# Gated delta rule: block inverses, key products and root chains in PSUM, banks regrouped, gated output in one product

## The chip, the cores and the metric

The kernel runs on one core of a Trainium2 chip. The metric is the device time of one execution in microseconds. A core has these engines: PE (matrix products, with a weight load, PEld, ahead of each), DVE (elementwise and reductions), ACT (activation functions and copies), POOL (elementwise) and SP (here only a queue that issues transfers). Each takes its instructions in the order in which the build wrote them down. Two memories are on the core: SBUF, and PSUM with eight banks of 512 fp32 values per partition. PE writes its results to PSUM; DVE and ACT read and write both memories, POOL and the transfers only SBUF.

## The reference

Four layers on 256 tokens of width 1024 in fp32. The change lies in the first layer's mixer, a gated delta rule with 8 key heads and 16 value heads of 128, in chunks of 64 tokens:

```
q = silu(conv(h @ w_q)); k = ...; v = ...      # q, k: 8 heads, each used by 2 value heads
q, k = l2_norm(q), l2_norm(k)                  # x * rsqrt(sum(x*x) + 1e-6)
a = where(strict, (k*beta) @ k.T * decay, 0)
t_inv = triangular_solve(eye + a, eye)         # lower triangular, unit diagonal
u, w = t_inv @ (v*beta), t_inv @ (k*beta*exp(g))
qk = q @ k.T * decay
for each chunk:                                # scan over the chunks
    v_new = u_c - w_c @ state
    out = qd_c @ state + qk_c @ v_new
    state = state * exp(gl_c) + kd_c.T @ v_new
o = out * rsqrt(mean(out*out) + 1e-6) * out_gain * silu(z)
x = x + o @ w_out
```

## The kernel before

All weights are fp32 and stream in chunks of 128 x 1024. ACT rounds a chunk to its high part (wh, L465), then DVE (L470) or POOL (L468), as a fixed pattern in the stage's plan says, subtracts that from the raw chunk to get the low part (wl). Three products of high and low parts make one fp32 product on PE (L481 and L484, or L493 to L495).

A planner orders the instructions of each engine at build time, from the order of the program, priorities, its own estimates of durations, and the memory slots that are free. At run time the order is fixed. A tile pool is a set of slots; a tile that finds none free waits until the slot's last user is done.

The stage of the gated delta rule runs from the start to about 350 us. In program order: the z gates for the first group of four value heads; the small projections for beta and decay; `project` for k, then for q (four steps each: PE projects into the pool `acc`, four banks of PSUM, DVE convolves in three steps at L726, ACT applies silu, squares go to PE again, which sums them per head into the tile pss); `rsqrt` of the sums of k, 32 values per partition; `rb` = rk * beta, which PE transposes (ps_rk, L884) and which goes through DRAM to be a row on all partitions.

Key products: for two token halves n and two head groups b PE multiplies k by itself (ps_kk, L902), ACT scales each head into an SBUF tile kkn (L905), DVE multiplies it by the decay row into UU (L909). The diagonal blocks of 32 x 32 go through DRAM into a tile A that has one block per partition. `tri_inverse` inverts all 128 blocks at once on DVE, 31 rounds of two instructions, a product into stmp (L1826) and a subtraction from T (L1827):

```
for i in range(31):
    r, m = 31 - i, i // parts + 1
    tv = tmp[:, : r * m].rearrange("p (c j) -> p c j", c=r)
    V.tensor_tensor(tv, A[:, i, i + 1 :]..., T[:, i, :m]..., op=ALU.mult)
    V.tensor_tensor(T[:, i + 1 :, :m], T[:, i + 1 :, :m], tv, op=ALU.subtract)
```

T and its transpose return through DRAM (dTR). While DVE works on this, PE goes on with q, the key-query products (ps_kq, L961, scaled by ACT into kkn at L964, multiplied on DVE at L967), the v projections (`values`, with PE transposes ps_v at L943), and the z gates. A string in the plan gives the order of what follows, `+` for parts that alternate:

```
order='v0 z1 v1 z2 l0 v2 l1+s0 v3 l2+s1 z3 l3+s2 s3'
```

v are the values, z the gates, l the levels, which join the 32 x 32 inverses to blocks of 128 (`join_blocks`), s the scans with `out_norm` at their end. All of the tiles pss, ps_rk, ps_kk, ps_kq, ps_v and those of levels and scan share one PSUM pool with the tag `mm` and four banks. In `out_norm` POOL multiplies the gate zs by the scan's output (L1048) while DVE works out the rsqrt, and DVE scales each head (L1050). `_gdn_out` transposes that (ps_ot, L1073) and multiplies by w_out.

Of the kernel before, what the change touches and what calls it, by code (L numbers as in the profile page):

```python
# [41 lines left out]
        gk=4,  # L42
        tag='mm',
        order='v0 z1 v1 z2 l0 v2 l1+s0 v3 l2+s1 z3 l3+s2 s3',
# [331 lines left out]
def run(g):  # L376
    for _ in g:
        pass
# [3 lines left out]
class Prog:  # L382
# [114 lines left out]
    def rsqrt(self, out, src, shape, scale, eps, pool=None, tag=None, bufs=1, key=""):  # L497
# [18 lines left out]
        for i in range(3):  # L516
# [5 lines left out]
            nc.vector.scalar_tensor_tensor(out if i == 2 else y, t, 1.5, y, op0=ALU.add, op1=ALU.mult)  # L522

    def load_row(self, src, shift=None, queue=None):

        self.row = self.xp.tile([128, D + 128], F32, name="row", tag="row")
        queue = queue or self.nc.sync
        queue.dma_start(self.row[:, :D], src.partition_broadcast(128))
        if shift is not None:
            self.nc.gpsimd.memset(self.row[:, D:], 0.0)  # L530
            queue.dma_start(self.row[0:8, D:], shift)
# [197 lines left out]
    def gdn(self, x):  # L729
        nc, tc, ap = self.nc, self.tc, self.ap  # L730
        with ExitStack() as outer:
            self.psum(outer)
            for t in range(2):
                self.stats(x, t, [self.pa.tile([128, 512], F32, name="junk", tag="acc") for _ in range(2)])
            self.prefetch(*((self.ap["g_z"][c], CW) for c in range(self.plan["pre"])))
            self.load_first(outer, "fi0")
            dr = outer.enter_context(tc.tile_pool(name="g_dram", bufs=1, space=DRAM))
            go = outer.enter_context(tc.tile_pool(name="g_o", bufs=1, reuse_waits="tile"))
            vb = [[go.tile([128, 4, 128], F32, name=f"vb{n}{g}") for g in range(4)] for n in range(2)]
            zs = [[go.tile([128, 4, 128], F32, name=f"zs{n}{g}") for g in range(4)] for n in range(2)]  # L740
            rq = go.tile([128, 2, 16], F32, name="rq")
            inner = ExitStack()
            gi = inner.enter_context(tc.tile_pool(name="g_i", bufs=1, reuse_waits="tile"))
            scan_last = self._gdn_core(x, dr, gi, vb, rq, zs, inner)
            self._gdn_out(x, zs, scan_last, inner)

    def _gdn_core(self, x, dr, gi, vb, rq, zs, inner):
# [42 lines left out]

        run(gates(0))
        phase_a = ExitStack()
        pA = phase_a.enter_context(tc.tile_pool(name="g_a", bufs=1, reuse_waits="tile"))
# [34 lines left out]

        def project(dst, c0, mt0):

            pss = self.pm.tile([128, 2, 16], F32, name="pss", tag="mm")
            sqs = []
# [20 lines left out]
            sums()  # L853
            yield pss

        with tc.tile_pool(name="g_rk", bufs=1, reuse_waits="tile") as pr:
            rrow = pr.tile([16, S], F32, name="rrow")
            kp, qp = project(kc, 0, 8), project(qc, 4, 0)
            for _ in range(self.plan["gk"]):
# [18 lines left out]
            fl = lambda a: a.rearrange("p n h -> p (n h)")  # L878
            self.rsqrt(fl(rk), fl(next(kp)), (128, 32), 1.0, 1e-6, pool=pr)
            rb = pr.tile([128, 2, 16], F32, name="rb")  # L880
# [13 lines left out]
        for n in range(2):  # L894
# [3 lines left out]
            for b in range(2):  # L898
                ps = self.pm.tile([128, 4, 128], F32, name="ps_kk", tag="mm")
                for k in range(4):  # L900
                    a = kc[:, b * 4 + k, n * 128 : n * 128 + 128]
                    nc.tensor.matmul(ps[:, k, :], a, a, start=True, stop=True)  # L902
                kk = gi.tile([128, 4, 128], F32, name="kkn", tag="kkn", bufs=2)
                for k in range(4):
# [9 lines left out]
        for g in range(4):  # L914
            u = UU[:, 8 * g : 8 * g + 8]
            nc.gpsimd.affine_select(u, u, [[0, 8], [1, 128]], ALU.not_equal, 1.0, base=0, channel_multiplier=-1)

        A = pA.tile([128, 32, 32], F32, name="sA")
        T = pA.tile([128, 32, 32], F32, name="sT")
        tmp = pA.tile([128, 256], F32, name="stmp")  # L920
        nc.sync.dma_start(A.rearrange("p j c -> p (j c)"), dA)
        self.tri_inverse(128, A, T, tmp)
        nc.sync.dma_start(dTR[0], T.rearrange("p c j -> p (c j)"))
        nc.vector.tensor_copy(A, T.rearrange("p c j -> p j c"))
        nc.sync.dma_start(dTR[1], A.rearrange("p c j -> p (c j)"))

# [22 lines left out]
        with tc.tile_pool(name="g_rq", bufs=1, reuse_waits="tile") as pr:  # L949
            for _ in range(3):  # L950
                next(qp)
            next(v0)
            self.rsqrt(fl(rq), fl(next(qp)), (128, 32), 1.0, 1e-6, pool=pr)
            nc.vector.tensor_scalar(rq, rq, 128.0 ** -0.5, None, op0=ALU.mult)
            nc.vector.tensor_tensor(rq2, rq, rq, op=ALU.mult)
        for n in range(2):
            for b in range(2):
                ps = self.pm.tile([128, 4, 128], F32, name="ps_kq", tag="mm")
                for k in range(4):
                    sl = (slice(None), b * 4 + k, slice(n * 128, n * 128 + 128))  # L960
                    nc.tensor.matmul(ps[:, k, :], kc[sl], qc[sl], start=True, stop=True)  # L961
                kq = gi.tile([128, 4, 128], F32, name="kkn", tag="kkn", bufs=2)
                for k in range(4):
# [5 lines left out]

        pB = inner.enter_context(tc.tile_pool(name="g_b", bufs=1, reuse_waits="tile"))  # L970
        TR = [pB.tile([128, 2, 8, 128], F32, name=f"TR{i}") for i in range(2)]
        E = pB.tile([128, 8, 64], F32, name="lev_e")
        for t in (*TR, E):
            nc.gpsimd.memset(t, 0.0)
        t2k = lambda nm: pB.tile([128, 4, 128], F32, name=nm, tag="b2k", bufs=5)
        TG = self.plan["tag"]
        bank = lambda nm, tag="mm": self.pm.tile([128, 4, 128], F32, name=nm, tag=tag)
        def mm4(lhs, rhs, nm, tag="mm"):
            ps = bank(nm, tag)
            for u in range(4):  # L980
# [16 lines left out]
        def scan(g):  # L997
            hs = slice(4 * g, 4 * g + 4)
            bc = lambda c: c.unsqueeze(2).to_broadcast([128, 4, 128])

            vn = t2k("vn")
            nc.scalar.copy(vn, mm4(TR[g % 2][:, 1, 0:4], vb[0][g], "ps_vn", TG))
            kd = t2k("kd")
            ps = bank("ps_kd", TG)
            for i in range(2):
# [4 lines left out]
            st = t2k("st")  # L1010
            nc.scalar.copy(st, mm4(kd, vn, "ps_s", TG))
            nc.scalar.copy(vb[0][g], mm4(GT[0][:, hs], vn, "ps_o", TG))
            yield

            ps = bank("ps_ks", TG)
            for i in range(2):
# [3 lines left out]
            nc.gpsimd.tensor_tensor(vb[1][g], vb[1][g], ks, op=ALU.subtract)  # L1020
            ps = bank("ps_qs", TG)
            for i in range(2):
# [4 lines left out]
            vn1 = t2k("vn")  # L1027
            nc.scalar.copy(vn1, mm4(TR[g % 2][:, 1, 4:8], vb[1][g], "ps_vn", TG))
            yield
            nc.vector.tensor_tensor(vb[1][g], mm4(GT[1][:, hs], vn1, "ps_o", TG), qs, op=ALU.add)  # L1030
            yield
# [3 lines left out]
        def out_norm(g):  # L1035

            hs = slice(4 * g, 4 * g + 4)
            for n in range(2):
# [8 lines left out]
                nc.vector.tensor_tensor(rs, rs, rq[:, n, hs], op=ALU.mult)  # L1047
                nc.gpsimd.tensor_tensor(zs[n][g], zs[n][g], o, op=ALU.mult)  # L1048
                for u in range(4):
                    nc.vector.tensor_scalar(zs[n][g][:, u, :], zs[n][g][:, u, :], rs[:, u : u + 1], None, op0=ALU.mult)  # L1050

# [1174 lines left out]
```

## Time and profile before

| | |
|---|---|
| median of three runs | 1629.03 us (1623.34 to 1630.67) |
| profiled execution: its time, its span | 1627.05 us, 1625.3 us |
| busy over the span | PE 91%, PEld 80%, DVE 72%, ACT 50%, POOL 41% |
| chain that ended last, by engine | PE 52%, DVE 17%, issue 4%, DMA 4% |
| mean granted clock of PE | 0.957 |

A share over the span is a mean over stages with different limits. [...] An instruction is written as engine, line, operation, out<-in. "Releaser" is what ended an engine's idle time.

### The profile page before, as it was taken

The numbers are of one execution on the slowest core, as the hardware profiler recorded it, in microseconds if no ns is written. First come the engines' busy times: TensorE is split into PE (matmuls) and PEld (weight loads), VectorE is DVE, ScalarE is ACT, GpSimd is POOL, SyncE is SP. The second block draws the span as 40 slices with busy tenths as digits, with TensorE's granted clock in tenths as the row PEclk, the third lists the DMA queues.
The fourth block names the chain that finished last, engine by engine and source line by source line (L and its number), as shares of the span: only waits on it lengthen the run. The fifth ranks groups of instructions, "written<-read, shape, count | busy, mean of one in ns | idle before, by whom it ended". The sixth has DMA issues, their size and how long they took to land.

```text
span 1625.3 us, 25792 instructions
## 1 busy us (share of the span) xinstructions
PE 1472.6 (91%) x9586; PEld 1300.0 (80%) x9586; DVE 1172.8 (72%) x2346; ACT 815.8 (50%) x1478; POOL 674.4 (41%) x441
## 2 busy tenths in 40 slices
PE   5778798899999899999998798999798879899998
PEld 4777687779998787999877576799787767589987
DVE  4478856877777766887566787788976769776652
ACT  4744344554444465555345356555545436466651
POOL 4544553416544342335136413265535521335630
PEclk9898899999999999999999899999999889899999
DMA  4554442258777444888633313677774331265551
GB/s 167 163 154 140 141 115 83 71 199 326 276 292 280 157 130 147 301 328 321 248 114 114 116 66 104 227 276 258 264 257 147 110 114 66 105 223 195 181 196 40
DMA packets 103246, 292.96 MB, mean 180 GB/s; under 512 B 28072, under 2 KB 37968, under 8 KB 96976
## 3 DMA queue, kind: packets, MB, share of 16 engines
q1 hardware_dynamic: 93872, 237.12, 43.0%
q10 hardware_dynamic: 8896, 53.14, 9.0%
q8 instruction: 75, 1.23, 0.3%
q0 software_dynamic: 352, 1.06, 0.2%
q14 instruction: 51, 0.42, 0.1%
HBM read 288.04 MB, written 3.24 MB: 179 GB/s over the span
## 4 chain that ended last, share of the span: by engine, by line
PE 52%; DVE 17%; issue 4%; DMA 4%; ACT 3%; POOL 2%; SPq 0%; ACTq 0%; DVEq 0%; POOLq 0%
PE ps_gu L481 14%; PE ps_gu L484 7%; PE ps_o L493 6%; PE ps_o L495 6%; PE ps_o L494 6%; DVE wl L470 3%; DVE gu_u L2180 1%; DVE a_AT L1827 1%; DVE ada_raw L1350 1%; DMA ada_raw<-in_ada 1%; DMA raw<-in_u_gu 1%; DVE a_stmp L1826 1%; ACT wh L465 1%; PE ps_u L481 1%; DMA a_AT<-a_dA 1%
## 5 line engine op out<-in xcount | busy, mean ns | idle before, releaser
L468 POOL TENSOR_TENSOR wl<-raw,wh 128x1024 fp32r<-128x1024 f32 (+4 forms) x162 | 401.3, 2485 | 457.4 <-ACT wh L465 411.2
L465 ACT CAST wh<-raw 128x1024 fp32r<-128x1024 f32 (+3 forms) x421 | 422.8, 1018 | 256.2 <-PE ps_o L494 95.8
L470 DVE TENSOR_TENSOR wl<-raw,wh 128x1024 fp32r<-128x1024 f32 (+2 forms) x259 | 347.1, 1350 | 126.7 <-ACT wh L465 126.4
L481 PE MATMUL ps_gu<-h_hi,wh 128*128 128x256 f32 x1280 | 313.0, 283 | 9.4 <-DVE gu_u L2180 9.4
L481 PE MATMUL ps_gu<-h_lo,wh 128*128 128x256 f32 x1280 | 312.4, 283 | 0.0
L481 PEld LDWEIGHTS ps_gu<-h_hi,wh 128*128 128x128 f32 x1280 | 244.6, 191 | 10.3 <-issue 10.1
L481 PEld LDWEIGHTS ps_gu<-h_lo,wh 128*128 128x128 f32 x1280 | 244.7, 191 | 0.2
L1350 DVE CUSTOM_DVE_ANT_0 ada_raw<-ada_raw,ada_cond 128x1024 f32<-128x1024 f32 x96 | 174.1, 1829 | 60.0 <-DMA ada_raw<-in_ada 60.0
L484 PE MATMUL ps_gu<-h_hi,wl 128*128 128x256 f32 x1280 | 177.9, 282 | 3.6 <-POOL wl L468 3.5
L484 PEld LDWEIGHTS ps_gu<-h_hi,wl 128*128 128x128 f32 x1280 | 163.0, 190 | 4.2 <-POOL wl L468 3.9
L495 PE MATMUL ps_o<-wl,act_h 128*128 128x512 f32 x352 | 138.8, 394 | 0.0
L494 PE MATMUL ps_o<-wh,act_l 128*128 128x512 f32 x352 | 138.5, 394 | 0.0
L493 PE MATMUL ps_o<-wh,act_h 128*128 128x512 f32 x352 | 138.4, 393 | 0.0
L2180 DVE SCALAR_TENSOR_TENSOR gu_u<-ps_gu,f2s,gu_u 128x254 f32<-128x254 f32 (+1 forms) x176 | 81.4, 477 | 40.8 <-ACT gu_u L2178 38.8
L711 POOL TENSOR_TENSOR act_l<-gu_t,act_h 128x256 fp32r<-128x256 f32 x44 | 54.9, 1250 | 115.0 <-ACT act_h L710 110.8
L2183 POOL TENSOR_TENSOR gu_t<-gu_t,gu_u 128x256 f32<-128x256 f32 x44 | 48.8, 1108 | 86.1 <-DVE gu_u L2180 80.5
L495 PEld LDWEIGHTS ps_o<-wl,act_h 128*128 128x128 f32 x352 | 66.1, 188 | 15.4 <-issue 0.5
L494 PEld LDWEIGHTS ps_o<-wh,act_l 128*128 128x128 f32 x352 | 66.1, 188 | 15.1 <-issue 0.2
L493 PEld LDWEIGHTS ps_o<-wh,act_h 128*128 128x128 f32 x352 | 66.1, 188 | 15.0 <-issue 0.2
L481 PE MATMUL ps_g<-h_hi,wh 128*128 128x256 f32 x256 | 69.4, 303 | 0.2 <-ACT wh L465 0.2
L481 PE MATMUL ps_g<-h_lo,wh 128*128 128x256 f32 x256 | 68.9, 301 | 0.0
L710 ACT CAST act_h<-gu_t 128x256 fp32r<-128x256 f32 x44 | 17.7, 407 | 98.4 <-DVE gu_t L709 98.4
(648 smaller groups left out, 3068.0 us busy)
## 6 DMA issues: line engine op xcount, KB each, us to landing
ada_raw<-in_ada ACTq DMA_DIRECT2D x48, 1024.0 KB, 6.1
raw<-in_f_gu SPq DMA_DIRECT2D x88, 512.0 KB, 5.0
raw<-in_u_gu SPq DMA_DIRECT2D x88, 512.0 KB, 4.3
raw<-in_f_dn SPq DMA_DIRECT2D x44, 512.0 KB, 4.6
raw<-in_u_dn SPq DMA_DIRECT2D x44, 512.0 KB, 4.1
raw<-in_g_qkv SPq DMA_DIRECT2D x32, 512.0 KB, 3.7
raw<-in_g_z SPq DMA_DIRECT2D x16, 512.0 KB, 3.5
raw<-in_g_out SPq DMA_DIRECT2D x16, 512.0 KB, 3.9
```

Of the source, the lines that this page charges most:

```text
L465: self.last_copy = nc.scalar.copy(wh[:, :cols], raw[:, :cols])
L468: nc.gpsimd.tensor_tensor(wl[:, :cols], raw[:, :cols], wh[:, :cols].bitcast(F32), op=ALU.subtract)
L470: nc.vector.tensor_tensor(wl[:, :cols], raw[:, :cols], wh[:, :cols].bitcast(F32), op=ALU.subtract)
L481: nc.tensor.matmul(ps, wh[:, k * width + m0 : k * width + m0 + m], xx[:, k, :], start=(n == 0), stop=(n == last))
L484: nc.tensor.matmul(ps, wl[:, k * width + m0 : k * width + m0 + m], xh[:, k, :], start=False, stop=(n == last))
L493: nc.tensor.matmul(ps, xh, wh[:, sl], start=start, stop=False, **kw)
L494: nc.tensor.matmul(ps, xl, wh[:, sl], start=False, stop=False, **kw)
L495: nc.tensor.matmul(ps, xh, wl[:, sl], start=False, stop=stop, **kw)
L711: nc.gpsimd.tensor_tensor(al[:, m, :], t, ah[:, m, :].bitcast(F32), op=ALU.subtract)
L1350: nc.vector.tensor_tensor_reduce(raw[:, j], raw[:, j], self.cond, 1.0, 0.0, op0=ALU.mult, op1=ALU.add, accum_out=mod[:, i : i + 1])
L2180: nc.vector.scalar_tensor_tensor(u[:, j, d:], ps[:, j, : S - d], cw[:, 3 * q + 2 - d : 3 * q + 3 - d], u[:, j, d:], op0=ALU.mult, op1=ALU.add)
L2183: nc.gpsimd.tensor_tensor(t, t, u[:, 0], op=ALU.mult)
```

## The change

1. `tri_inverse` in this stage gets T as a tile of two PSUM banks. ACT copies the result to SBUF for the first store through DRAM; DVE's transposing copy reads PSUM.
2. The scaled key products stay in the PSUM bank of the products (`kk = ps`, `kq = ps`); ACT writes them in place, and the SBUF tile kkn goes.
3. `rsqrt_p` takes the place of `rsqrt` for the sums of k and q: its sums and three working arrays lie in one PSUM bank, the estimate y in SBUF. It has 12 steps in place of 11.
4. The pool `mm` has two banks in this stage in place of four. The other two are, one after the other, a pool for the k sums and the key products (`pe`), the tile T (`pt`), and a pool of the scan's own (`pscan`).
5. `out_norm` multiplies gate, scale and output in one DVE instruction per head; POOL's product goes.

```
-            self.psum(outer)
+            self.psum(outer, 2)
...
+    def rsqrt_p(self, out, ws, n, eps, pool):
+        V = self.nc.vector
+        src, v, hv, t = ws
+        V.tensor_scalar(v, src, eps, None, op0=ALU.add)
+        V.tensor_scalar(hv, src, -0.5, -0.5 * eps, op0=ALU.mult, op1=ALU.add)
+        seed = pool.tile([128, n], I32, name="rs_s")
+        V.tensor_scalar(seed, v.bitcast(I32), -0.5, float(0x5F3759DF), op0=ALU.mult, op1=ALU.add)
+        y = seed.bitcast(F32)
+        for i in range(3):
+            V.tensor_tensor(t, hv, y, op=ALU.mult)
+            V.tensor_tensor(t, t, y, op=ALU.mult)
+            V.scalar_tensor_tensor(out if i == 2 else y, t, 1.5, y, op0=ALU.add, op1=ALU.mult)
...
+        early = ExitStack()
+        pe = early.enter_context(tc.tile_pool(name="g_pe", bufs=2, space=PSUM, reuse_waits="tile"))
...
-            pss = self.pm.tile([128, 2, 16], F32, name="pss", tag="mm")
+            both = pool.tile([128, 4, 32], F32, name="pss", tag=tag)
+            pss = both[:, 0].rearrange("p (n h) -> p n h", n=2)
...
-            kp, qp = project(kc, 0, 8), project(qc, 4, 0)
+            kp, qp = project(kc, 0, 8, pe, "e"), project(qc, 4, 0, self.pm, "mm")
...
-            self.rsqrt(fl(rk), fl(next(kp)), (128, 32), 1.0, 1e-6, pool=pr)
+            ws = next(kp)
+            self.rsqrt_p(fl(rk), [ws[:, i] for i in range(4)], 32, 1e-6, pr)
...
-                ps = self.pm.tile([128, 4, 128], F32, name="ps_kk", tag="mm")
+                ps = kk = pe.tile([128, 4, 128], F32, name="ps_kk", tag="e")
...
-                kk = gi.tile([128, 4, 128], F32, name="kkn", tag="kkn", bufs=2)
...
+        early.close()
         A = pA.tile([128, 32, 32], F32, name="sA")
-        T = pA.tile([128, 32, 32], F32, name="sT")
+        sT = pA.tile([128, 32, 32], F32, name="sT")
...
-        self.tri_inverse(128, A, T, tmp)
-        nc.sync.dma_start(dTR[0], T.rearrange("p c j -> p (c j)"))
-        nc.vector.tensor_copy(A, T.rearrange("p c j -> p j c"))
-        nc.sync.dma_start(dTR[1], A.rearrange("p c j -> p (c j)"))
+        with tc.tile_pool(name="g_pt", bufs=1, space=PSUM, reuse_waits="tile") as pt:
+            T = pt.tile([128, 32, 32], F32, name="psT")
+            self.tri_inverse(128, A, T, tmp)
+            nc.scalar.copy(sT, T)
+            nc.sync.dma_start(dTR[0], sT.rearrange("p c j -> p (c j)"))
+            nc.vector.tensor_copy(A, T.rearrange("p c j -> p j c"))
+            nc.sync.dma_start(dTR[1], A.rearrange("p c j -> p (c j)"))
...
-                kq = gi.tile([128, 4, 128], F32, name="kkn", tag="kkn", bufs=2)
+                kq = ps
...
+        pscan = inner.enter_context(tc.tile_pool(name="g_ps", bufs=2, space=PSUM, reuse_waits="tile"))
...
-        bank = lambda nm, tag="mm": self.pm.tile([128, 4, 128], F32, name=nm, tag=tag)
+        bank = lambda nm: pscan.tile([128, 4, 128], F32, name=nm, tag="scan")
...
-                nc.gpsimd.tensor_tensor(zs[n][g], zs[n][g], o, op=ALU.mult)
                 for u in range(4):
-                    nc.vector.tensor_scalar(zs[n][g][:, u, :], zs[n][g][:, u, :], rs[:, u : u + 1], None, op0=ALU.mult)
+                    nc.vector.scalar_tensor_tensor(zs[n][g][:, u, :], zs[n][g][:, u, :], rs[:, u : u + 1], o[:, u, :], op0=ALU.mult, op1=ALU.mult)
```

The q sums' rsqrt is replaced in the same way as that of k.

## Rows read from the trace of the kernel before

**Rows 1.** PE's waits, 60 to 206 (last: 136 to 140): total us, times, longest.
```profile
PE ps_v L943 <- ACT v L727: 15.2, 4, 8.5
PE ps_rk L884 <- DVE rb L881: 5.0, 1, 5.0
PE ps_kq L961 <- ACT qc L727: 3.9, 1, 3.9
...
PE ps_v L943 <- ACT v L727: 2.6, 1, 2.6
```

**Rows 2.** Timeline of DVE from 159 us: start us, us, engine, line.
```profile
171.24 0.42 DVE L1827 TENSOR_TENSOR sT<-sT,stmp 128x255 f32<-128x255 f32 x1
171.69 2.47 DVE L1826 TENSOR_TENSOR stmp<-sA,sT 128x256 f32<-128x256 f32 x1
```

**Rows 3.** Timeline of POOL, 159 to 176 us.
```profile
171.31 2.57 POOL L468 TENSOR_TENSOR wl<-raw,wh 128x1024 fp32r<-128x1024 f32 x1 [2.22 <-ACT wh L465]
```

**Rows 4.** Lines L726, L909: count: ns min/median/max, first to last start.
```profile
L726 DVE SCALAR_TENSOR_TENSOR cv_y<-ps_g,fi,cv_y x96: 460/479/486, 46.8 to 254.0; 128x255 f32<-128x255 f32 x32, 128x254 f32<-128x254 f32 x32, 128x253 f32<-128x253 f32 x32
...
L909 DVE TENSOR_TENSOR UU<-kkn,row x8: 679/680/2829, 106.9 to 119.4; 128x512 f32<-128x512 f32 x8
```

**Rows 5.** Windows: length, busy us by engine, PE clock, DMA, GB/s.
```profile
90.00:100.00 10.00, 6.04 (x38) 5.99 (x39) 5.40 (x17) 5.51 (x15) 1.40 (x1) 0.66 0.60 173
...
120.00:130.00 10.00, 8.92 (x64) 8.92 (x64) 8.30 (x18) 5.80 (x16) 3.41 (x4) 0.83 0.90 236
...
150.00:160.00 10.00, 9.09 (x35) 7.37 (x36) 9.22 (x17) 4.11 (x6) 6.20 (x2) 0.83 0.37 117
...
180.00:190.00 10.00, 7.21 (x19) 5.34 (x20) 9.14 (x22) 3.60 (x7) 2.36 (x1) 0.50 0.41 146
```

**Rows 6.** DVE's groups in the stage: count, busy us, mean ns, idle.
```profile
L909 DVE TENSOR_TENSOR UU<-kkn,row 128x512 f32<-128x512 f32 x8 | 10.8, 1402 | 0.0
L1826 DVE TENSOR_TENSOR stmp<-sA,sT 128x31 f32<-128x31 f32 (+15 forms) x31 | 22.3, 721 | 0.7
L1827 DVE TENSOR_TENSOR sT<-sT,stmp 128x31 f32<-128x31 f32 (+15 forms) x31 | 16.6, 537 | 0.7
...
L521 DVE SCALAR_TENSOR_TENSOR rs_t<-rs_t,rs_v 128x32 f32<-128x32 f32 x6 | 5.0, 830 | 0.1
L520 DVE TENSOR_TENSOR rs_t<-rs_s 128x32 f32<-128x32 f32 x6 | 3.3, 558 | 0.1
L522 DVE SCALAR_TENSOR_TENSOR rq<-rs_t,rs_s 128x32 f32<-128x32 f32 x1 | 2.3, 2291 | 0.0
```

**Rows 7.** DVE's groups by shape, over the span (same columns).
```profile
L1254 DVE TENSOR_TENSOR qr<-ps_ro,sT 128x256 f32<-128x256 f32 x4 | 1.7, 425 | 2.8 <-PE ps_ro L1253 2.8
...
L1826 DVE TENSOR_TENSOR stmp<-sA,sT 128x31 f32<-128x31 f32 x2 | 0.4, 188 | 0.0
```

**Rows 8.** Timeline of DVE, 1008 to 1024 us: two steps through PSUM.
```profile
1009.96 0.70 DVE L644 TENSOR_TENSOR ps_o<-ps_o,grow 128x512 f32<-128x512 f32 x1 [2.13 <-PE ps_o L495]
1010.70 0.69 DVE L645 TENSOR_TENSOR x_t<-ps_o,x_t 128x512 f32<-128x512 f32 x1
```

**Rows 9.** Timeline of all engines, 196 to 209 us.
```profile
196.84 1.13 DVE L924 COPY sA<-sT 128x1024 f32<-128x1024 f32 x1
...
206.73 0.22 PE L1700 MATMUL ps_e<-TR,UU 128*32 128x32 f32 x2 [1.74 <-DMA TR<-dTR]
```

**Rows 10.** Timelines from 100 us (DVE) and from 316 us (all).
```profile
106.85 4.30 DVE L909 TENSOR_TENSOR UU<-kkn,row 128x512 f32<-128x512 f32 x4
...
326.87 2.73 DVE L1077 SCALAR_TENSOR_TENSOR ol<-ps_ot,fi,oh 128x512 fp32r<-128x512 f32 x4
```

**Rows 11.** Tile ps_kk: its matmuls (columns as in rows 4).
```profile
L902 PE MATMUL ps_kk<-kc x32: 275/335/417, 94.3 to 99.4; 128*128 128x128 f32 x32
```

**Rows 12.** Costliest groups of the page, POOL's gated product.
```profile
L1048 POOL TENSOR_TENSOR zs<-zs,vb 128x512 f32<-128x512 f32 x8 | 10.3, 1287 | 25.4 <-ACT vb L1012 16.7 <-DVE vb L1030 8.7
```

**Rows 13.** Line L1050 (columns as in rows 4).
```profile
L1050 DVE TENSOR_SCALAR zs<-zs,g_rs x32: 273/282/2426, 232.9 to 325.5; 128x128 f32<-128x128 f32 x32
```

More of the change, by code (lines that the diff above doesn't have):

```diff
@@ L42 @@
         gk=4,
-        tag='mm',
         order='v0 z1 v1 z2 l0 v2 l1+s0 v3 l2+s1 z3 l3+s2 s3',
@@ L827, in _gdn_core, with project @@
         sel = self.fcol("sel").rearrange("p (k m) -> p k m", k=8)
-        def project(dst, c0, mt0):
-            pss = self.pm.tile([128, 2, 16], F32, name="pss", tag="mm")
+        def project(dst, c0, mt0, pool, tag):
+            both = pool.tile([128, 4, 32], F32, name="pss", tag=tag)
+            pss = both[:, 0].rearrange("p (n h) -> p n h", n=2)
             sqs = []
@@ L853, in project @@
             sums()
-            yield pss
+            yield both
         with tc.tile_pool(name="g_rk", bufs=1, reuse_waits="tile") as pr:
             rrow = pr.tile([16, S], F32, name="rrow")
-            kp, qp = project(kc, 0, 8), project(qc, 4, 0)
+            kp, qp = project(kc, 0, 8, pe, "e"), project(qc, 4, 0, self.pm, "mm")
             for _ in range(self.plan["gk"]):
@@ L952, in _gdn_core @@
             next(v0)
-            self.rsqrt(fl(rq), fl(next(qp)), (128, 32), 1.0, 1e-6, pool=pr)
+            ws = next(qp)
+            self.rsqrt_p(fl(rq), [ws[:, i] for i in range(4)], 32, 1e-6, pr)
             nc.vector.tensor_scalar(rq, rq, 128.0 ** -0.5, None, op0=ALU.mult)
@@ L975, in _gdn_core, with mm4 @@
         t2k = lambda nm: pB.tile([128, 4, 128], F32, name=nm, tag="b2k", bufs=5)
-        TG = self.plan["tag"]
-        bank = lambda nm, tag="mm": self.pm.tile([128, 4, 128], F32, name=nm, tag=tag)
-        def mm4(lhs, rhs, nm, tag="mm"):
-            ps = bank(nm, tag)
+        bank = lambda nm: pscan.tile([128, 4, 128], F32, name=nm, tag="scan")
+        def mm4(lhs, rhs, nm):
+            ps = bank(nm)
             for u in range(4):
@@ L1001, in scan @@
             vn = t2k("vn")
-            nc.scalar.copy(vn, mm4(TR[g % 2][:, 1, 0:4], vb[0][g], "ps_vn", TG))
+            nc.scalar.copy(vn, mm4(TR[g % 2][:, 1, 0:4], vb[0][g], "ps_vn"))
             kd = t2k("kd")
-            ps = bank("ps_kd", TG)
+            ps = bank("ps_kd")
             for i in range(2):
@@ L1010, in scan @@
             st = t2k("st")
-            nc.scalar.copy(st, mm4(kd, vn, "ps_s", TG))
-            nc.scalar.copy(vb[0][g], mm4(GT[0][:, hs], vn, "ps_o", TG))
+            nc.scalar.copy(st, mm4(kd, vn, "ps_s"))
+            nc.scalar.copy(vb[0][g], mm4(GT[0][:, hs], vn, "ps_o"))
             yield
-            ps = bank("ps_ks", TG)
+            ps = bank("ps_ks")
             for i in range(2):
@@ L1020, in scan @@
             nc.gpsimd.tensor_tensor(vb[1][g], vb[1][g], ks, op=ALU.subtract)
-            ps = bank("ps_qs", TG)
+            ps = bank("ps_qs")
             for i in range(2):
@@ L1027, in scan @@
             vn1 = t2k("vn")
-            nc.scalar.copy(vn1, mm4(TR[g % 2][:, 1, 4:8], vb[1][g], "ps_vn", TG))
+            nc.scalar.copy(vn1, mm4(TR[g % 2][:, 1, 4:8], vb[1][g], "ps_vn"))
             yield
-            nc.vector.tensor_tensor(vb[1][g], mm4(GT[1][:, hs], vn1, "ps_o", TG), qs, op=ALU.add)
+            nc.vector.tensor_tensor(vb[1][g], mm4(GT[1][:, hs], vn1, "ps_o"), qs, op=ALU.add)
             yield
```

## The prediction

> **What bounds the kernel now.** I read the page first. In its chain that ended last most of the span is PE's and the next share DVE's, so an edit gains only where PE stands still, or where it works at the lower clock. The edits all lie in the first stage, the gated delta rule, from 0 to about 350 us. Next I read PE's waits there. Between 60 and 206 us PE waits 5.0 us for rb, 3.9 us for the key-query products, and 15.2 us in four pieces for the transposes of v (tile ps_v); one of these four, 2.6 us at 136, stands apart [rows 1]. Each of these waits leads back to DVE: rb is the end of the rsqrt chain for k, and the transposes and the products wait for a convolution whose three steps (L726) queue on DVE behind other work.
>
> Then I asked why DVE is late. A step of the block inverse on 255 elements takes 0.42 us, the next one, on 256, takes 2.47 us [rows 2]. Over the same stretch POOL runs a weight subtraction, from 171.31 to 173.88 [rows 3]; DVE's long step starts in it and ends just behind it. So a DVE instruction with two SBUF operands stands still while POOL works on SBUF. The convolution steps, which read one operand from PSUM and one from SBUF, never do: 96 of them take 460 to 486 ns, with POOL busy much of that time. The key products, with two SBUF operands, reach from 679 to 2829 ns [rows 4].
>
> [...]
>
> **What the change takes from DVE.** Block inverse: 62 steps take 22.3 and 16.6 us [rows 6]. Unstretched, 31 elements take 0.188 us and 256 take about 0.425 [rows 7], so 0.155 us and 1.05 ns an element. The 31 steps of a line work on r(32-r) elements for r from 1 to 31, 5,456 in all: 31 x 0.155 + 5.7 = 10.5 us a line, 21.1 for both. Stretch: 38.9 - 21.1 = 17.8 us. Key products: 8 x (1.402 - 0.680) = 5.8 us [rows 4, 6]. rsqrt chains of k and q: an unstretched step on 32 elements is 0.155 + 0.034 = 0.19 us, so 6 x (0.83 - 0.19) + 6 x (0.56 - 0.19) + (2.29 - 0.19) = 8.2 us, about half in each chain [rows 6]. In sum 31.8 us of standing still go, if a PSUM operand frees the step. In all these new forms at most one tensor operand lies in SBUF.
>
> **What a PSUM operand costs.** Lower bound nothing: 256 elements with one PSUM input take 425 ns, which is what 255 from SBUF take [rows 2, 7]; an output in PSUM costs 0.70 against 0.69 us, and a step that needs it starts 0.04 us behind its end, as between the SBUF steps (171.66 to 171.69) [rows 2, 8]. Upper bound: the convolution step on 255 elements is 0.48 us, 0.06 more than the inverse's, though it is another operation with a scalar pointer [rows 4]. For 62 + 24 steps that is 0 to 5 us. I take 20 ns a step, 1.7 us, as the tensor products are the nearer row. [...]
>
> **What PE gets back.** The k chain: 4.1 us come free ahead of rb, whose wait is 5.0; the new chain has one step more, so 1.1 us stay. Key products: 5.8 us free before a wait of 3.9, which goes. Transposes of v at 148, 173 and 184: 15.2 - 2.6 = 12.6 us of waits, with 17.8 us plus the q chain's 4.1 coming free; these go too. The wait at 136 stays: there DVE works unstretched. Gross 5.0 + 3.9 + 12.6 = 21.5 us. Clock: busy time by the missing share, 6.04 x 0.34 + 8.92 x 0.17 + 9.09 x 0.17 + 7.21 x 0.50 = 8.7 us [rows 5]. Ceiling 30.2 us.
>
> Does the inverse itself come early enough? DVE's copy behind its last step starts at 196.84, the first product that needs the inverse at 206.7, after a last wait of 1.74 us for the store and reload through DRAM [rows 9]. Those 10 us stay. PE's own way to 206 shortens in this part by 12.6 + 1.6 + 3.6 = 17.8 us; the inverse moves up by 17.8 + 4.1 - 1.7 = 20.2, less the new ScalarE copy of T, which DVE's copy may have to wait for (that one takes 1.13 us, and I take the same). So 19 against 17.8: neither outruns the other by much, and the copy is covered. While it waits for the last step, weight copies stand behind it on ScalarE, and weight loads behind the store of T on SP's queue, which that store heads already now; both run ahead of PE here, so I take nothing, and 1.1 us if they don't. The memset of T moves from the start to just before the inverse; DVE does it while A's trip through DRAM runs. [...]
>
> **What the banks cost.** The pool "mm" falls from four banks to two, and one of these is held by the q sums until their rsqrt is done. (a) Key products: all 32 matmuls start by 99.4 now; with two banks those of the second token half need the first half's DVE products, the first two of which end near 108, unstretched [rows 10, 11]. If PE's queue kept the place, PE would stand about 9 us; if the build's planner moves them behind projection work, nothing. (b) Key-query products: with one bank each of four waits for the scaling and two DVE products of the one before; the same 0 to 9 us. PE has z and v projections to do meanwhile, and the planner plans by free banks, so I take 2.5 us for each, nearer to the low end. (c) At the end of the stage the four transposed outputs need four banks' worth; the DVE steps that free them stand behind one another, 2.73 us for four [rows 10]: 0 to 2.7, taken 1.0. The scan gets two banks of its own. Each of its products already needs the copy of the one before, so nothing is taken for it.
>
> **Gated output.** Eight POOL products of 1.29 us go (10.3 us), with the 25.4 us for which they wait at the head of POOL's queue [rows 12]; weight subtractions queue behind them, but PE loses no listed time to those, so the gain is bounded by 0 and 10.3 and I take 0.5. On DVE 32 scalings of 282 ns become products with a scalar; from the convolution's 479 ns less 127 elements that is 0.345, so 2.0 us more over eight groups, most of it beside PE's projections; 0.5 taken, 2.0 if that cover is gone. They have two SBUF operands and can still stand behind POOL, as the scalings do (2426 at most) [rows 13].
>
> **Sum.** 30.2 - 1.1 (rest of the k chain) - 2.0 (clock behind waits that remain) - 2.5 - 2.5 - 1.0 (banks) + 0.5 - 0.5 = 21.1 us. The profiled execution took 1627.05 us, 1.75 above its span and 2.0 below the median of the runs (1629.03). 1627.05 - 21.1 = 1606 us, 1.3 to 1.4% faster. The later stages are the same code and are taken as unchanged; a planner that lays them out a little differently is worth a few us either way.
>
> **Rivals.** (1) The banks take back more than half: (a) to (c) near their upper ends, 9 + 9 + 2.7 less the 6 already taken, 15 us: gain 3 to 13, 1614 to 1624. For it: PE's queue is fixed at build, and two banks were in use where four were. Against: PE has other work there. Chance 0.14. (2) No change: PE's waits only change their name, because something else comes as late as DVE did (the weights' copies, or the convolution's ScalarE steps), or because steps with PSUM operands stand behind POOL too. Against: the listed waits for weights are small, and the 96 convolution steps have no long one. 1621 to 1635, chance 0.12. (3) Slower: the one free bank under the q sums. If PE's queue holds the key-query products ahead of the v and z projections, PE stops at each turn of the bank, and each stop is followed by the lower clock. It decides where these stops pass 26 us in all: over 6 us at each of four turns with 2 us of clock behind each, 32 us, gives 1627 - 26 + 32 = 1633; up to 1640. Chance 0.06. [...] The rows on tensor products speak against it; 0.06. The forecast, 1595 to 1614, keeps 0.62.
>
> **Range and chances.** What a measurement here can tell from no change is about 0.5%, 8 us. Faster by more: 0.62 + 0.06 + 0.10 of (1) = 0.78; within: 0.04 of (1) + 0.10 of (2) = 0.14; slower 0.06 + 0.02 = 0.08. The range is from 1595, nothing lost of the ceiling and a little more, to 1621, where two thirds of (1) are still in; it leaves out about 0.2.
>
> **What would show it.** Right: no block-inverse step above 0.6 us, their sum near 21 to 23 us; key products at 0.68; rb's wait near 1 us; ps_v's waits near 3 us in place of 15.2; a granted clock near 1.0 around 180; the first product on the inverse some 30 us earlier than 206.7, less the bank waits. Wrong: inverse steps of 2 us still; PE waiting on a DVE product or a ScalarE scaling before ps_kk, ps_kq or ps_ot for more than 6 us; or the gain lost again between 206 and 350.

## The result, and the profile after

The changed kernel takes 1600.99 us (median of four runs, 1599.26 to 1608.05) against 1629.85 for the kernel before in the same rounds: ratio 0.9836, 95% interval 0.9802 to 0.9871. The profiled executions stand at 1627.05 and 1601.26 us, 25.8 apart; the forecast was 21.1 with a range of 1595 to 1621. One execution of j1 below, the profiled one, ran at a mean granted clock of 0.83 of full speed, where the others have 0.95 or more, and took 1665.62 us; j1's ratio leaves it out, and its profile is not read. In the new numbering the inverse is at L1848 and L1849, the convolution at L740, the weight subtraction at L467 (POOL) and L469 (DVE).

PE's waits after the change, 60 to 206 us, as in [rows 1]:

```profile
...
PE ps_kq L984 <- DVE pss L535: 3.6, 1, 3.6
PE ps_e L1722 <- DMA TR<-dTR: 1.4, 1, 1.4
PE ps_kk L921 <- ACT kc L741: 1.4, 1, 1.4
PE ps_kk L921 <- DVE UU L927: 1.2, 1, 1.2
PE ps_rk L903 <- DVE rb L900: 1.2, 1, 1.2
PE ps_kk L921 <- DVE rk L536: 0.9, 1, 0.9
PE ps_v L965 <- DVE psT L1849: 0.7, 1, 0.7
```

The 15.2 us for ps_v are 0.7. Three waits for ps_kk are new or were short: 3.5 us in all. The wait for ps_kq is nearly as long as before, 3.6 against 3.9, but it is no longer for the convolution. The profile names a step of the q chain on the tile pss as its releaser; yet that chain uses its bank up to 131.84, and PE goes on at 130.96, just behind the second DVE product on the ps_kq before (L990, until 130.81):

```profile
130.13 0.68 DVE L990 TENSOR_TENSOR GT<-ps_kq,GT 128x512 f32<-128x512 f32 x1
130.73 0.19 DVE L535 TENSOR_TENSOR pss<-pss,rs_s 128x32 f32<-128x32 f32 x1
...
131.65 0.19 DVE L536 SCALAR_TENSOR_TENSOR rq<-pss,rs_s 128x32 f32<-128x32 f32 x1
```

```profile
130.96 2.62 PE L984 MATMUL ps_kq<-qc,kc 128*128 128x128 f32 x16 [3.65 <-DVE pss L535]
```

So the q sums hold one of the pool's two banks, and PE waits for the other: case (b) of the prediction.

DVE's groups in the same stretch, as in [rows 6] (count, busy us, mean ns, idle before):

```profile
L1849 DVE TENSOR_TENSOR psT<-psT,stmp 128x31 f32<-128x31 f32 (+15 forms) x31 | 10.7, 346 | 0.6
L1848 DVE TENSOR_TENSOR stmp<-sA,psT 128x31 f32<-128x31 f32 (+15 forms) x31 | 10.3, 333 | 0.5
...
L927 DVE TENSOR_TENSOR UU<-ps_kk,row 128x512 f32<-128x512 f32 x8 | 5.0, 684 | 0.1
...
L978 DVE TENSOR_TENSOR rq<-rq 128x32 f32<-128x32 f32 x1 | 2.3, 2314 | 0.0
L977 DVE TENSOR_SCALAR rq<-rq 128x32 f32<-128x32 f32 x1 | 2.2, 2174 | 0.0
L900 DVE TENSOR_TENSOR rb<-rk,bcol 128x32 f32<-128x32 f32 x1 | 1.7, 1710 | 0.0
...
L534 DVE TENSOR_TENSOR pss<-pss,rs_s 128x32 f32<-128x32 f32 x6 | 1.2, 195 | 0.1
```

The inverse fell from 38.9 to 21.0 us, the key products from 10.8 to 5.0. The root chains' steps take 0.19 us each. But rb and the two scalings of rq, which follow the chains with all operands in SBUF, now take 1.7 to 2.3 us. DVE's timeline around rb, and POOL's for the same microseconds, show what happened:

```profile
90.53 0.19 DVE L536 SCALAR_TENSOR_TENSOR rk<-pss,rs_s 128x32 f32<-128x32 f32 x1
90.75 1.71 DVE L900 TENSOR_TENSOR rb<-rk,bcol 128x32 f32<-128x32 f32 x1
```

```profile
85.36 7.05 POOL L467 TENSOR_TENSOR wl<-raw,wh 128x1024 fp32r<-128x1024 f32 x3 [3.02 <-ACT wh L464]
```

POOL works from 85.36 to 92.41. From 88.11 on the chain's steps, which have pss in PSUM, take 0.18 to 0.20 us each through that; rb, the first step without a PSUM operand, stands until 92.46, and the two steps behind it take 0.16 us each. So the standing still moved one instruction on.

The four windows of [rows 5]:

```profile
90.00:100.00 10.00, 7.94 (x67) 7.76 (x67) 5.85 (x15) 8.13 (x21) 4.89 (x4) 1.00 0.65 198
120.00:130.00 10.00, 7.32 (x54) 7.11 (x53) 5.80 (x18) 3.97 (x11) 4.22 (x4) 0.89 0.53 200
150.00:160.00 10.00, 10.00 (x84) 9.96 (x83) 8.69 (x20) 5.25 (x7) 6.50 (x4) 1.00 0.69 211
180.00:190.00 10.00, 8.57 (x73) 8.36 (x72) 4.33 (x9) 4.40 (x8) 9.97 (x6) 1.00 0.79 265
```

The granted clock is 1.00 in three of them and 0.89 in the fourth; PE is busy for all of the 40 us between 140 and 180. Over the stretches 0 to 60, 60 to 206 and 206 to 352 us, the kernel before and then the kernel after (PE busy is the second number, the granted clock the third from the end):

```profile
0.00:60.00 60.00, 40.89 (x248) 36.33 (x248) 31.02 (x53) 31.86 (x50) 26.41 (x17) 0.97 0.58 193
60.00:206.00 146.00, 111.08 (x717) 102.48 (x716) 110.69 (x182) 72.30 (x130) 74.54 (x33) 0.85 0.45 139
206.00:352.00 146.00, 132.33 (x1011) 113.98 (x1011) 98.90 (x224) 68.50 (x151) 58.03 (x36) 0.95 0.35 107
```

```profile
0.00:60.00 60.00, 40.20 (x242) 35.70 (x243) 30.00 (x51) 31.72 (x49) 25.87 (x17) 0.97 0.59 191
60.00:206.00 146.00, 128.34 (x1021) 120.13 (x1019) 96.93 (x211) 85.09 (x154) 81.60 (x39) 0.94 0.53 161
206.00:352.00 146.00, 129.48 (x872) 109.97 (x871) 104.12 (x230) 71.67 (x152) 46.71 (x26) 0.96 0.43 139
```

All of the gain is in the middle stretch: 17.3 us more of PE's work, at a clock of 0.94 in place of 0.85. The last stretch gained nothing. The stage has 1983 products on PE in both kernels; the changed one has 725 of them left at 206 us and takes 121 us for them, until the first product of the next stage (ps_gt, 327.0):

```profile
206.00:327.00 121.00, 106.07 (x725) 89.38 (x723) 87.48 (x203) 58.24 (x132) 37.81 (x21) 0.96 0.35 108
```

The kernel before comes to that point at 232 us and to ps_gt at 354.5, some 122 us later. One wait of the last stretch hangs on the gated product: its four pieces stand behind POOL's subtractions, the convolution for v queues behind them, and PE waits for that (POOL, DVE and PE from the timeline after 215 us):

```profile
215.17 2.39 POOL L467 TENSOR_TENSOR wl<-raw,wh 128x1024 fp32r<-128x1024 f32 x1 [1.62 <-PE ps_g L483]
...
215.22 5.47 DVE L1072 SCALAR_TENSOR_TENSOR zs<-zs,g_rs,vb 128x128 f32<-128x128 f32 x4
...
218.16 2.38 POOL L467 TENSOR_TENSOR wl<-raw,wh 128x1024 fp32r<-128x1024 f32 x1 [0.60 <-ACT wh L464]
...
224.74 0.69 PE L965 MATMUL ps_v<-ident,v 128*128 128x128 f32 x2 [4.13 <-ACT v L741]
```

### The profile page after: what moved, and what is told of

The parts are those of the page before. It is cut to its first block, busy times and chain, and to the rows that moved or that the text cites. A ratio compares the mean times of both kernels' runs of the same rounds, so it can differ in the third digit from the quotient of the medians.

```text
span 1599.6 us, 25783 instructions
## 1 busy us (share of the span) xinstructions
PE 1459.0 (91%) x9586; PEld 1289.3 (81%) x9586; DVE 1148.4 (72%) x2348; ACT 816.5 (51%) x1479; POOL 658.3 (41%) x433
## 3 DMA queue, kind: packets, MB, share of 16 engines
q8 instruction: 75, 1.23, 0.3%
## 5 line engine op out<-in xcount | busy, mean ns | idle before, releaser
L467 POOL TENSOR_TENSOR wl<-raw,wh 128x1024 fp32r<-128x1024 f32 (+4 forms) x162 | 395.0, 2445 | 449.8 <-ACT wh L464 378.8
L469 DVE TENSOR_TENSOR wl<-raw,wh 128x1024 fp32r<-128x1024 f32 (+2 forms) x259 | 346.6, 1348 | 126.7 <-ACT wh L464 122.0
L740 DVE SCALAR_TENSOR_TENSOR cv_y<-ps_g,fi,cv_y 128x253 f32<-128x253 f32 (+2 forms) x96 | 45.0, 478 | 34.8 <-ACT cv_y L738 33.3
```

The source lines that it names most:

```text
L467: nc.gpsimd.tensor_tensor(wl[:, :cols], raw[:, :cols], wh[:, :cols].bitcast(F32), op=ALU.subtract)
L469: nc.vector.tensor_tensor(wl[:, :cols], raw[:, :cols], wh[:, :cols].bitcast(F32), op=ALU.subtract)
```

## The experiments

All ratios are to the kernel before, in rounds on the same chip. Every kernel here computes all of the reference.

**One part undone at a time.** The first four kernels are the changed kernel with one part as it was: the inverse's T in SBUF, both root chains in SBUF, the scaled key and key-query products in SBUF, the gated output in two steps.

```
u1:  -            T = pt.tile([128, 32, 32], F32, name="psT")     +        T = sT
u2:  -            self.rsqrt_p(fl(rk), [...], 32, 1e-6, pr)       +  self.rsqrt(fl(rk), ws[:, 0], (128, 32), ...)   # rq too
u3:  -            ps = kk = pe.tile(...)   -  kq = ps             +  kk = gi.tile(..., name="kkn", ...)   # kq too
u4:  -            nc.vector.scalar_tensor_tensor(zs, zs, rs, o)   +  nc.gpsimd.tensor_tensor(zs, zs, o); nc.vector.tensor_scalar(zs, zs, rs)
```

u1_inverse_sbuf. 

> The changed kernel with one part undone: the block inverse keeps T in SBUF, as before; the two PSUM banks that T had stay empty meanwhile. Theory A (a DVE step with two SBUF operands stands behind POOL): the 62 steps go from 21.0 us back to 35 to 40 us, PE's waits for the transposes of v return (4.8 us to 12 or more), and the time is 1612 to 1620 us. Rival B (the gain is the regrouped banks and the order that the planner makes of them, the operands matter little): within 4 us of the changed kernel, 1597 to 1605 us.

u2_rsqrt_sbuf. 

> The changed kernel with the rsqrt of the k and q sums back in SBUF (the sums stay in the same PSUM bank). Theory A: the chains take about 8 us more between them, PE's wait for rb goes from 1.2 to 4 to 6 us, the clock falls behind it, time 1604 to 1610 us. On the other hand the bank of the q sums comes free after the first step and not after the whole chain, so PE's wait of 3.6 us for it goes; if that is as much as the chains cost, 1598 to 1603. Rival B: within 3 us of the changed kernel.

u3_products_sbuf. 

> The changed kernel with the scaled key products copied to SBUF again (kkn), so that a PSUM bank is free once ScalarE has read it. Theory A: the eight products into UU go from 0.68 us to 1.0 to 1.4 us each, 3 to 6 us of DVE, against which PE's waits for banks before the key products (2.4 us) and the key-query products (3.6 us) shrink; time 1599 to 1606 us. Rival B: the banks are what counts, so freeing them earlier gains: 1594 to 1599.

u4_gate_old. 

> The changed kernel with the gated output in its old form: POOL multiplies gate and output, DVE scales each head. Theory A: both forms can stand behind POOL; the new one loses 0.549 - 0.345 = 0.2 us in each of 32 steps and frees POOL of 10 us; undoing it gives 1598 to 1605 us, no difference that counts. Rival C (POOL's queue was blocked by its product, so this part carries a good share of the gain): 1606 us or more.

| | median us | ratio | interval |
|---|---|---|---|
| changed kernel | 1600.99 | 0.9836 | 0.9802 to 0.9871 |
| u1, inverse in SBUF | 1618.68 | 0.9954 | 0.9937 to 0.9972 |
| u2, root chains in SBUF | 1594.80 | 0.9803 | 0.9774 to 0.9832 |
| u3, products in SBUF | 1603.17 | 0.9854 | 0.9826 to 0.9882 |
| u4, gated output as before | 1603.84 | 0.9852 | 0.9819 to 0.9885 |

Only u1 stands apart from the changed kernel: without the inverse in PSUM 0.0118 of 1629 us, some 19 us, of the gain are gone. Its steps in SBUF took even longer than in the kernel before, 45.5 us (DVE's groups from 60 to 212 us, then two steps of DVE's timeline and POOL's for the same time):

```profile
L1846 DVE TENSOR_TENSOR stmp<-sA,sT 128x31 f32<-128x31 f32 (+15 forms) x31 | 26.8, 866 | 0.6
L1847 DVE TENSOR_TENSOR sT<-sT,stmp 128x31 f32<-128x31 f32 (+15 forms) x31 | 18.7, 604 | 0.6
```

```profile
159.06 2.63 DVE L1847 TENSOR_TENSOR sT<-sT,stmp 128x240 f32<-128x240 f32 x1
161.72 2.50 DVE L1846 TENSOR_TENSOR stmp<-sA,sT 128x247 f32<-128x247 f32 x1
```

```profile
159.01 4.94 POOL L467 TENSOR_TENSOR wl<-raw,wh 128x1024 fp32r<-128x1024 f32 x2 [0.25 <-ACT wh L464]
```

Two subtractions on POOL held up one DVE step each, by some 2.1 us; the next step took 0.42 us again. So the price went here by the POOL instructions that the chain met, not by its own steps. u3 and u4 show 2 to 3 us, which is less than their intervals can tell. In u4 the old scalings stand behind POOL as long as the new product does, and PE waits as long for the convolution behind them:

```profile
218.99 6.20 DVE L1073 TENSOR_SCALAR zs<-zs,g_rs 128x128 f32<-128x128 f32 x4
```

```profile
229.24 0.55 PE L965 MATMUL ps_v<-ident,v 128*128 128x128 f32 x2 [4.87 <-ACT v L741]
```

u2 came out below the changed kernel, by 0.0033, which the intervals do not separate, and below both forecasts for it; two further runs took that up.

**The banks alone, and the banks with the inverse.** b1 has the pools and tags of the changed kernel and every computation as before; b2 has the inverse in PSUM besides.

```
b1:  u1 + u2 + u3 + u4
b2:  u2 + u3 + u4
```

b1_banks_only. 

> The regrouped banks alone: the pools and tags of the changed kernel, with the block inverse, the key products, both reciprocal-root chains and the gated output done as in the kernel before (all SBUF). Theory A (the gain is VectorE's two-SBUF-operand steps no longer standing still behind GpSimd; the banks give nothing by themselves): 1622 to 1636 us, ratio 0.995 to 1.005, the inverse near 39 us or above, waits for ps_v 15 us or more. Rival B (a good part of the 27 us comes from the banks: separate pairs for the early products and the scan, the order of the work around them): 1612 us or less, ratio under 0.991.

b2_banks_inverse. 

> The regrouped banks and the block inverse in PSUM; key products, root chains and gated output as in the kernel before. Theory A: most of the gain is here, 1602 to 1614 us, ratio 0.985 to 0.992, inverse near 21 us; the parts left out (key products about 3 us dearer, gated output about 3, root chains about 5 cheaper, as the three runs with one part undone gave them) nearly cancel, so that the likeliest is 1602 to 1606. Rival C (the parts only pay together, because each wait that is removed shows the next): over 1614 us.

b1 took 1622.58 us, 0.9985 (0.9963 to 1.0008): the banks are worth nothing by themselves. b2 took 1604.86 us, 0.9869 (0.9836 to 0.9903): one part more, and 0.0116, again 19 us, are there. Theory A holds in both (b1's inverse takes 37.0 us and its waits for ps_v 13.3, a little less than was said), and rivals B and C fall. Between b2 and the changed kernel lies 0.0033, three parts together, not told apart from nothing.

**POOL kept quiet in the kernel before.** If a DVE step stands still only because POOL works on SBUF, the same steps must run at full speed with T in SBUF as soon as POOL has nothing to do. c1 is the kernel before with one line of the stage's plan changed, so that DVE makes all low parts of the weights:

```
-        w='PPPVPPPPPVPPPPPVPPPPPVPPPPPVPPPPPVPPPPPVPPPPPVPPPPVPPPVPPPVVVVVVV',
+        w='V',
```

c1_no_pool_sub. 

> The kernel before with one line changed: all low parts of this stage's weights are subtracted on VectorE, none on GpSimd; the inverse stays in SBUF. Theory A (steps with two SBUF operands are held up by GpSimd's subtractions, not by reading and writing SBUF as such): the inverse's 62 steps fall from 39 us to 20 to 24 with no step much over 0.5 us, though T never leaves SBUF. Rival D (a step in PSUM is by itself cheaper than one in SBUF): the inverse stays near 39 us. The time decides nothing here, since VectorE takes on some 50 subtractions: 1600 to 1650 us.

c1_timed. 

> The kernel before with all low parts of this stage's weights subtracted on VectorE, now timed in rounds (its one look gave 1573.5 us, with the inverse at 21.0 us in SBUF): 1568 to 1580 us, ratio 0.964 to 0.972.

A single execution took 1573.51 us, the timed runs 1577.61 us, 0.9705 (0.966 to 0.975). DVE's groups of c1_no_pool_sub from 60 to 206 us:

```profile
L470 DVE TENSOR_TENSOR wl<-raw,wh 128x1024 fp32r<-128x1024 f32 x36 | 44.4, 1233 | 4.8 <-ACT wh L465 4.7
...
L1827 DVE TENSOR_TENSOR sT<-sT,stmp 128x31 f32<-128x31 f32 (+15 forms) x31 | 10.5, 339 | 0.2
L1826 DVE TENSOR_TENSOR stmp<-sA,sT 128x31 f32<-128x31 f32 (+15 forms) x31 | 10.5, 338 | 0.2
...
L909 DVE TENSOR_TENSOR UU<-kkn,row 128x512 f32<-128x512 f32 x8 | 5.0, 680 | 0.0
```

The inverse takes 21.0 us in SBUF, as much as in PSUM after the change, and the key products 5.0. Theory A is shown, and rival D falls: PSUM made no step cheaper, it let the step pass POOL. The rows agree, with 0.42 us free and 2.47 us behind a POOL instruction of 2.57 [rows 2, 3]. What in SBUF holds the step, no run here shows.

The time was forecast at 1600 to 1650 and came out far better, at nearly twice the gain of the change. The stretches of c1_timed say where:

```profile
0.00:60.00 60.00, 47.23 (x314) 42.84 (x315) 37.40 (x70) 37.40 (x59) 2.71 (x7) 1.00 0.67 221
60.00:206.00 146.00, 134.91 (x1027) 124.36 (x1026) 118.84 (x236) 84.57 (x152) 11.57 (x10) 0.93 0.53 160
206.00:352.00 146.00, 136.94 (x1003) 119.45 (x1003) 114.67 (x254) 77.78 (x163) 48.30 (x31) 1.00 0.54 178
```

Against before PE does 6.3 us more work in the first stretch, 23.8 more in the second and 4.6 more in the third. The first has nothing to do with the inverse: at 10 us POOL makes the first three low parts in 7.05 us, where DVE takes 1.23 us for one. These stretches are equal in time, not in work: the stage's 1983 products are done at 354.5 us before and at 302.4 in c1_timed, again by the first ps_gt. Up to there, before and then c1_timed:

```profile
0.00:354.50 354.50, 285.64 (x1983) 253.96 (x1983) 242.91 (x462) 173.98 (x333) 158.98 (x84) 0.91 0.43 136
```

```profile
0.00:302.40 302.40, 271.07 (x1983) 241.53 (x1983) 231.16 (x510) 173.98 (x334) 37.64 (x36) 0.97 0.52 159
```

The 48 subtractions that moved cost DVE some 60 us (48 x 1.25), and yet it is busy 11.7 us less over the same stage (231.2 against 242.9). So some 70 us of its busy time before were steps standing still, an estimate from these figures; POOL was rid of 121 us of work.

**The change on a quiet POOL.** The same line in the changed kernel (c2), and in u2 (c3):

c2_after_no_pool_sub. 

> The changed kernel with the same one line: no subtraction of this stage on GpSimd. Theory A (what the change gains is only that VectorE's steps no longer stand still behind GpSimd): there is hardly anything left to gain once GpSimd is quiet, so 1566 to 1578 us, within 0.5% of the kernel before with that line. Rival G (steps in PSUM, the banks and the one-product gate each save work by themselves): the two gains add, 1573 less 20 to 27, 1545 to 1556 us.

c3_roots_sbuf_no_pool_sub. 

> The changed kernel with both root chains back in SBUF and no subtraction of this stage on GpSimd. Theory E (a chain in PSUM holds a bank that the products wait for, and with GpSimd quiet buys nothing): 2 to 5 us under the changed kernel with the quiet GpSimd, wait for ps_kq under 1 us. Rival H (the 5 us of the earlier run with both chains in SBUF was where the other work happened to fall): no difference, or slower.

| | POOL subtracts | DVE subtracts all |
|---|---|---|
| kernel before | 1629.85 | 1577.61, 0.9705 (0.966 to 0.975) |
| changed kernel | 1600.99, 0.9836 | 1582.12, 0.9737 (0.9701 to 0.9774) |
| changed, root chains in SBUF | 1594.80, 0.9803 | 1574.05, 0.9691 (0.9654 to 0.9729) |

With POOL quiet the change gains nothing; if anything it costs 4.5 us, which the intervals don't separate. Rival G (1545 to 1556 us) falls. Theory A's difference from c1 (0.5%) was met, its 1566 to 1578 us missed by 4. So what the change gains is time behind POOL, and the plan's one line takes the cause away, and more. What a saving on DVE would be worth here beyond that can't be read from these runs, as PE is at work for 131 of the 146 us of c2's middle stretch. c1 and c3 beat both kernels; the intervals don't tell these two apart. Theory E's 2 to 5 us between c2 and c3 came out as 8, with intervals that overlap.

**The root chains.** i1 is the changed kernel with only the q chain in SBUF, j1 with only the k chain.

```
i1:  -  self.rsqrt_p(fl(rq), [...], 32, 1e-6, pr)   +  self.rsqrt(fl(rq), ws[:, 0], (128, 32), 1.0, 1e-6, pool=pr)
j1:  -  self.rsqrt_p(fl(rk), [...], 32, 1e-6, pr)   +  self.rsqrt(fl(rk), ws[:, 0], (128, 32), 1.0, 1e-6, pool=pr)
```

i1_q_chain_sbuf. 

> The changed kernel with only the query's root chain back in SBUF (as before), the key's chain still in PSUM. Theory E (what the root chains in PSUM cost is the bank of the query's sums, held until the chain ends, for which the products of queries and keys wait): 1593 to 1597 us, 4 to 8 us under the changed kernel, the wait for ps_kq down from 3.6 to under 1 us, the wait for rb staying near 1.2 us. Rival F (it is the key's chain that costs, through the order of the steps): no better than the changed kernel, 1599 to 1603 us.

j1_k_chain_sbuf. 

> The changed kernel with only the key's root chain back in SBUF, the query's left in PSUM: the counterpart of the run with only the query's chain moved back, which gained nothing (ratio 0.9882 against 0.9836 of the changed kernel). Theory K (it is the key's chain in PSUM that costs): 1592 to 1598 us, like the run with both chains in SBUF. Rival N (neither chain is worth what single runs can tell; the 6 us of the run with both are within what the order of the work around them scatters): 1599 to 1605 us, like the changed kernel; the wait for ps_kq stays near 3.6 us.

i1 took 1604.56 us, 0.9882 (0.9844 to 0.9919); j1 took 1596.81 us, 0.9804 (0.9772 to 0.9836), the same as u2 with both chains in SBUF. Theory E falls: in i1 the wait for ps_kq is down from 3.6 to 1.7 us, and the time is no shorter. The intervals of i1 and j1 just miss each other, so it is better to have the k chain in SBUF than the q chain. Against the changed kernel neither j1's interval stands apart nor u2's, nor c3's against c2's. That all three lean the same way, by 5 to 8 us, speaks for theory K and does not show it. What u2's profile shows: rb stands still no longer, but one step of the chain does, so that PE's wait for ps_rk is 3.8 us there against 1.2. That is the wrong way round; the gain must come later. PE from 110 to 130 us, in the changed kernel and in u2:

```profile
110.00:120.00 10.00, 8.41 (x65) 8.01 (x64) 9.50 (x18) 6.70 (x20) 5.74 (x2) 0.94 0.45 64
120.00:130.00 10.00, 7.32 (x54) 7.11 (x53) 5.80 (x18) 3.97 (x11) 4.22 (x4) 0.89 0.53 200
```

```profile
110.00:120.00 10.00, 9.73 (x81) 9.37 (x79) 9.38 (x11) 6.20 (x14) 6.55 (x3) 1.00 0.63 172
120.00:130.00 10.00, 9.87 (x82) 9.63 (x82) 6.62 (x17) 7.29 (x21) 8.18 (x6) 1.00 0.86 250
```

PE does 3.9 us more there. The planner, which lays the engines' instructions anew for every edit, put a weight subtraction of DVE at 112 us in u2, between the key products, and at 118 in the changed kernel. Whether that order is the cause was not tried alone, and stays open.

## Why the prediction was right, step by step

**DVE stands still behind POOL, and a PSUM operand frees the step: right.** It is shown from both sides, by the inverse in PSUM under a busy POOL (21.0 us) and in SBUF under a quiet one (21.0 us). But it is not the count of SBUF operands that decides in these rows: L1848 reads one tensor from SBUF and writes another, and runs free, at 333 ns on average; L977 does the same and stood for 2.17 us. What the first has and the second lacks is a tensor in PSUM. The inverse's 21.1 unstretched microseconds were met within 0.1, the key products' 5.4 within 0.4.

**The price of a PSUM operand: 20 ns a step were taken, 0 to 5 us as bounds.** Between c1 in SBUF and the changed kernel in PSUM a product went from 338 to 333 ns and a subtraction from 339 to 346. So it is the lower bound, and the chance of 0.06 that was given to dearer PSUM steps did not come true in these 62.

**The root chains: this term was wrong.** 8.2 us were to go. The chains' steps did come down, but rb and the two rq scalings, which I had left out since they had not been stretched before, took over 5.6 us of it (6.2 less three free steps of 0.19). u2 shows that nothing was gained. My own argument had it: if POOL holds up the step that has all its tensors in SBUF, a chain in PSUM that ends in such a step only shifts the stop. So it was: rb took 1.71 us and the scalings 2.17 and 2.31, where c1_timed, with POOL quiet, has 0.19, 0.18 and 0.18.

**What PE gets back.** rb's wait: 1.1 us were to stay, 1.2 did. ps_v: 15.2 fell to 0.7, where 2.6 were to stay; PE comes to the first transposes 3 us later (138.2 against 135.0). The clock: windows at 1.00, 0.89, 1.00 and 1.00, as forecast; in the kernel before it was 0.50 from 91 to 97, 122 to 125, 153 to 155 and 177 to 189 us (windows of 1 us), late in PE's stops from 89, 117, 148 and 173 us or behind them. The wait for the key-query products did not go, it became a wait for a bank (above).

**The first product on the inverse.** The working of the prediction has 19 us here and its list of signs about 30; the two do not agree. It was 18.2 (188.53 against 206.73), so the working was right and the list wrong. DVE's copy behind the last step comes 20.5 us earlier, where 20.2 were worked out, or 19 with a wait for ACT's copy of T. That wait was an estimate which no row of before shows; DVE's copy started 0.03 us behind the end of ACT's (176.33), after 0.17 us of waiting:

```profile
176.36 1.22 DVE L946 COPY sA<-psT 128x1024 f32<-128x1024 f32 x1 [0.17 <-ACT sT L944]
```

```profile
188.53 0.22 PE L1722 MATMUL ps_e<-TR,UU 128*32 128x32 f32 x2 [1.43 <-DMA TR<-dTR]
```

From the copy to the product it is 12.2 us in place of 9.9: the first reload is issued at 184.22, right behind POOL's memset of TR (182.37, 1.82 us), which has POOL's subtractions ahead of it. PE has done more by then, 1032 products up to 190 us against 873, and is never idle from 140 to 180; it still waits 1.4 us for the reload, as it waited 1.7 before.

**The banks: 2.5, 2.5 and 1.0 us were taken.** The waits for ps_kk are 3.5 us, 1.4 of them for a convolution and not for a bank; for ps_kq 3.6, for ps_ot 1.3. Each is near what was taken and far from its upper end, as argued: PE has projection work in between. Rivals (1) and (3) fall, and b1 puts the banks in sum at 0.9985, not told apart from nothing.

**The gated output: mis-sized.** I took 0.5 us off and on, 2.0 at most. DVE's busy time for it between 206 and the stage's end rose from 11.2 to 15.6 us, and PE's wait of 4.1 us at 224 hangs on it. But the old form is busy for 15.3 us in u4, so the form is not what costs. In steps that were not held up the new one takes 347 ns against 282 (medians of the changed kernel and the kernel before), 2 us over all 32, as worked out; the rest of the rise is time behind POOL, which either form pays there. u4 is no better: POOL's product costs nothing that the runs can tell.

**The sum.** 25.8 us by the profiled executions against 21.1. The first stage ends 27.5 us earlier (the first ps_gt at 327.0 against 354.5), the later stages gave 1.7 back. Between 60 and 206 us PE's listed waits fell from 33.8 to 17.5 us, 16.3 less. The clock gave back 9.0 us by the prediction's measure, busy time by the missing share (111.08 x 0.15 less 128.34 x 0.06), where 6.7 were taken; the 2.6 us for ps_v went as well. About 19 of the 27 to 29 us are the inverse alone, where the ceiling had 17.8 (12.6 of waits, 5.2 of clock): that part was foreseen. For the rest the sum has 12.4 us of gains less 9.1, a net of 3.3, and the runs show some 5, not told apart from nothing (b2 against the changed kernel). That these two are near is luck: the wait for ps_kq did not go, and u2, where PE waits 3.8 us for rb again, is no slower.

What I did not see was the larger finding: the rows that showed DVE waiting for POOL also named the cheaper cure. [rows 3] has a POOL subtraction of 2.57 us; on DVE it is 1.23. I costed only what the change does to the waiting engine, not what the other one was doing there.

## What to carry to other kernels

When an elementwise step is six times its usual length, look at the other engine's timeline for the same microseconds before moving any data: here, with SBUF operands on both sides, some 70 us of VectorE's time, by the estimate above, went with 121 us of GpSimd's work. Ask first whether that work can leave GpSimd (0.9705 here); only then which steps may pass it with a tensor in PSUM (0.9836), and then take the whole run of steps up to the next wait, as the stop moved here to the first one left behind (rb, 1.71 us). This change was worth 1.6%, and nothing once its cause was gone (0.9737 against 0.9705), so try the two together before keeping both.

## What was not expected of the hardware

- One subtraction of 128 x 1024 took 2.4 us on GpSimd (2.39 at 215 us in the changed kernel) and 1.2 on VectorE (1.23 in c1_no_pool_sub); with 48 of them moved to VectorE, its busy time up to the end of the stage fell, from 242.9 to 231.2 us, and the kernel took 3% less.
- GpSimd's instructions held up one step each: in u1 two of them, 4.94 us in all, held up one step to 2.63 us and the next to 2.50. Of the short steps from rb on only the first stood until GpSimd was done (1.71 us at rb, then 0.16 and 0.16).
- ACT's copy of T from PSUM (175.32, 1.01 us) and DVE's (176.36, 1.22 us) ran one after the other, as the forecast had it. DVE's copy waited 0.17 us for ACT's; whether the two could share a bank was not tried.
